# Where the attention scores of ten heads stand in TensorE's order: in front of the previous head's value products

## The chip, the core and the metric

The kernel runs on one core of a Trainium2 chip. A core has five engines, each with an instruction stream of its own that it works through in order: TensorE (PE in the profile, with its weight loads shown apart as PEld), VectorE (DVE), ScalarE (ACT), GpSimd (POOL) and SyncE (SP). TensorE multiplies, VectorE and ScalarE do the elementwise work, and in this kernel SyncE issues the loads of the weights while GpSimd issues the small transfers that turn data around. Engines wait for each other by semaphores. The metric is the device time of one execution in microseconds, lower is better.

## The reference

The kernel computes one decoder layer on a sequence of 256 tokens and 2048 channels, in float32. Cut to what matters here:

```python
h = rmsnorm(x)                                     # 256 x 2048
q_a, c_kv, k_rope, z_mla, c_in, b_gate, c_gate, z_conv, g_mla, g_conv = split(h @ w_in)
q = rmsnorm(q_a) @ w_q_b                           # 16 heads x (128 + 64 rotary)
kv = rmsnorm(c_kv) @ w_kv_b                        # 16 heads x (128 key + 128 value)
sc = (q_nope @ k_nope.T + q_rope @ k_rope.T) / sqrt(192)
attn = softmax(causal(sc)) @ v                     # per head, 256 x 128
attn = attn * silu(z_mla)
conv = short_conv(c_gate * c_in, 3 taps)
y_conv = (b_gate * conv * silu(z_conv)) @ w_o_conv
merged = sigmoid(g_mla) * (attn @ w_o_mla) + sigmoid(g_conv) * y_conv
out = x + rmsnorm(merged @ w_out)
```

## The kernel before

Every product is made of three passes: each float32 operand is split into a high part (`hi`) and the rest (`lo`), and `hi*hi`, `hi*lo` and `lo*hi` are added in PSUM. So every weight that arrives (tile `raw`) is first split: ScalarE copies it into `whi` (line 243), and VectorE subtracts to get `wlo` (line 244). Both steps are `split_act`, and the same function splits the queries, keys, values and probabilities.

The weights come as units of 128 x 2048 elements, in one list in the order in which they are used. `take(i)` hands unit i to the matmuls and has unit i+1 split. The halves of the split units live in five rotating buffers for `whi` and five for `wlo`, so the split of a half waits until TensorE has read the half five places before.

The middle of the program is a loop over the 16 heads h. `at = h % 4` is the place of a head among four and `v = h // 4` counts those fours. What TensorE does in one head, in order:

- if `at` is 0: four units of the gate `z` for these four heads (`gates`). From the second four on, the probabilities of the head before are brought in and split during the second of these units (`turn`), and during the third come that head's value products (`values(h - 1, pt)`) and the values of the next four heads (`make("v", v)`);
- the scores of head h, `score(h)` (line 812; for head 0 after the first `channels` unit, for the last head within the head before, line 824);
- `channels(h, 0)` and `channels(h, 1)`: two of the four units of a 512-column block of the convolution branch, which has nothing to do with the attention. They accumulate in two PSUM banks with the tag `cv`;
- `turn(h - 1)` (split of the previous head's probabilities, no matmul), `channels(h, 2)`, and `values(h - 1, pt)`;
- `make(...)`: in an even head the rotary queries of the next two heads (`group_r`), in an odd head their queries and keys (`group_a`, tiles `qn` and `kn`; one buffer each, for two heads);
- `channels(h, 3)`, after which `channels_done` empties the two `cv` banks. In heads with `at` 1 this is a VectorE instruction for each bank (line 716), in heads with `at` 0 and 2 one of ScalarE (lines 714 and 718).

A score is eight short matmuls (lines 607 to 613). The first of them multiplies the query by the keys' high and low parts together:

```python
mm(o, qn[0][:, j, t0], kn[:, :, j, :P], start=True, stop=False)
```

After the scores comes the softmax of that head: ScalarE copies half of the scores out of PSUM (line 618), VectorE adds the halves and the mask and finds the maxima (lines 619 to 627), ScalarE takes exponentials (line 630), VectorE divides and transposes blocks of 32 x 32 (lines 634 to 637, and 318 in `turned`). Then four transfers of GpSimd's queue write the tile to memory in turned order (`go`, line 326), and one brings it back (`come`, line 330). `come` isn't issued at once but put on the list `coming`; `arrive()` takes the oldest entry from the list and issues it. GpSimd issues its transfers in program order, so one that waits holds up those behind it.

`group_a` ends in this, for the keys: TensorE's result goes through `whole` (ScalarE line 393, VectorE line 394) to the tile `f`, and `split_act` makes `kn` from it (ScalarE line 243 for the high part, VectorE line 244 for the low part).

All matmuls stay in the order in which the program gives them (the wrapper `matmul`), and so does whatever stands in `tc.keep_in_program_order`. All other instructions, among them most of VectorE's and ScalarE's, are put in order by a scheduler at build time, which goes by its own estimate of when each would be ready. So a change in the program's order can move instructions on engines that the change doesn't name.

ScalarE holds the table of one set of functions at a time. The exponential of the softmax and the sigmoid of the gates need different ones, and where one follows the other the build puts a table load in between.

Of the kernel before, what the change touches and what calls it, by code (L numbers as in the profile page):

```python
# [23 lines left out]
H = 16  # L24
# [58 lines left out]
def tile_layer(ctx: ExitStack, tc: tile.TileContext, xw, w0, xb, x, pos, pvec, post_g, wc, wz, wcv, wkr, wqk, wqr, wv, cwr, wsq, out):  # L83
# [129 lines left out]
    def take(i):  # L213
        ahead(i)
        parts = splits.pop(i)

        def piece(j, n):
            o = j * n
            h, o = o // HALF, o % HALF
            return parts[h][0][:, o : o + n], parts[h][1][:, o : o + n]  # L220

        return piece

    def bank(name, tag="mm", bufs=4):
        return psum.tile([P, 512], F32, name=name, tag=tag, bufs=bufs)
# [80 lines left out]
    def temp(name, shape=(P, S), dt=F32, bufs=2, tag=None):  # L306

        tag, n = tag or name.rstrip("0123456789_"), shape[-1]
        if n % LINE == 0:
            return bp.tile(list(shape), dt, name=name, tag=tag, bufs=bufs)  # L310
        return bp.tile([P, -(-n // LINE) * LINE], dt, name=name, tag=tag, bufs=bufs)[:, :n]
# [78 lines left out]
    def whole(dst, ps):  # L390

        t = temp("half")
        nc.scalar.activation(t[:, :], ps[:, S:], AF.Copy)
        nc.vector.tensor_tensor(dst, ps[:, :S], t[:, :], op=ALU.add)
# [98 lines left out]
    def latent_split(name, both, g):  # L493

        f = lat_f[name].rearrange("p t (i k x) -> p k t i x", i=4, k=KR)
        for k in range(KR):
            hi, lo = (both[:, k, o : o + S].rearrange("p (t i x) -> p t i x", t=NT, i=4) for o in (0, S))
            tc.keep_in_program_order(nc.scalar.activation(hi, f[:, k], AF.Copy, scale=col(g, k)))
            tc.keep_in_program_order(
                nc.vector.scalar_tensor_tensor(lo, f[:, k], col(g, k), hi.bitcast(F32), op0=ALU.mult, op1=ALU.subtract)  # L500
            )
# [33 lines left out]
    def key_rope():  # L535
        rows(kr_f)
        rope(kr_f, kr_f, True)
        split_act(kr[:, 0, :], kr[:, 1, :], kr_f)
# [57 lines left out]
    def make(i, j):  # L596
        {"a": group_a, "r": group_r, "v": group_v}[i](j)
# [44 lines left out]
    def turn(p):  # L642

        pt = temp("pt", (P, 2, 3 * P), F32R, 1)
        hi, lo = (pt[:, j : j + 1, :].rearrange("p o (k q) -> p (o k) q", k=3) for j in range(2))
        split_act(quarters(hi), quarters(lo), by_rows(p[:, :], 3), True)
        return pt

    def values(h, pt):
        vv = groups["v", h // HV]  # L650
        j = h % HV
        o = bank(f"o{h}", tag="o", bufs=1)
        vs = slice(j * DV, (j + 1) * DV)
        both = o[:, :].rearrange("p (i q) -> p i q", i=2)
        mm = matmul
        mm(both, vv[0][:, 0, vs], pt[:, :, :S], start=True, stop=False)
        mm(o[:, :S], vv[1][:, 0, vs], pt[:, 0, :S], start=False, stop=False)
        mm(o[:, P:S], vv[1][:, 1, vs], pt[:, 0, S:], start=False, stop=False)
        mm(both[:, :, P:], vv[0][:, 1, vs], pt[:, :, S:], start=False, stop=True)

        at = at_t[:, h // HV, :, :].rearrange("p t (i k x) -> p t i k x", i=4, k=HV)[:, :, :, j, :]
        f = temp("f")
        whole(f[:, :], o)
        nc.vector.tensor_tensor(at, f[:, :].rearrange("p (t i x) -> p t i x", t=NT, i=4), at, op=ALU.mult)
# [5 lines left out]
    def quarter(pss, w, i):  # L670

        for t in range(NT):
            for k4 in range(4):
                k = 4 * i + k4
                a = [x_both[:, k, o + t * P : o + (t + 1) * P] for o in (0, S)]
                product(pss[t][:, :], a, w(k4, 512), k == 0, k == KD - 1)

    def gates(v, i):
        if i == 0:
            z_ps["now"] = [bank(f"z{v}_{t}") for t in range(NT)]  # L680
        quarter(z_ps["now"], take(u_gate[v][i]), i)

    def gates_done(v):
        for t in range(NT):
            ps, g, r = z_ps["now"][t], at_t[:, v, t, :], r_col[:, t : t + 1]
            nc.scalar.activation(g, ps[:, :], AF.Sigmoid, scale=r)
            now = nc.vector.scalar_tensor_tensor(g, ps[:, :], r, g, op0=ALU.mult, op1=ALU.mult)
            if v == 0:
                tc.keep_in_program_order(now)

    def gates_turn(v, t):
        g = at_t[:, v, t, :]
        go, come = turned(g, temp("cw", (P, 512), bufs=2), 4)
        go()
        return lambda: come(g)
# [5 lines left out]
    def channels(h, i):  # L701

        if i == 0:
            cv_ps["now"] = [bank(f"cv{h}_{t}", tag="cv", bufs=2) for t in range(NT)]
        quarter(cv_ps["now"], take(u_head[h][i]), i)
        if i == 3:
            channels_done(*divmod(h, 4))

    def channels_done(j, n):
        for t in range(NT):  # L710
            ps, r = cv_ps["now"][t], r_col[:, t : t + 1]
            w, u = cv_w[:, t, :], cv_t[:, j, t, :]
            if n == 0:
                nc.scalar.activation(u, ps[:, :], AF.Copy, scale=r)
            elif n == 1:
                nc.vector.scalar_tensor_tensor(u, ps[:, :], r, u, op0=ALU.mult, op1=ALU.mult)
            elif n == 2:
                nc.scalar.activation(w, ps[:, :], AF.Copy, scale=r)
            else:
                g = temp("cg", (P, 512), bufs=1)  # L720
                nc.scalar.activation(g[:, :], ps[:, :], AF.Sigmoid, scale=r)
                nc.vector.scalar_tensor_tensor(g[:, :], ps[:, :], r, g[:, :], op0=ALU.mult, op1=ALU.mult)
                nc.vector.tensor_tensor(w, w, g[:, :], op=ALU.mult)
# [48 lines left out]
    def arrive():  # L772
        coming.pop(0)()

    def score(h):
        ps_by_head[h], come = scores(h)
        coming.append(come)

    for h in range(H):
        v, at = divmod(h, HV)  # L780

        if at == 0:
            for i in range(4):
                gates(v, i)
                if v == 0 and i == 0:
                    ckv_come()
                elif v == 0 and i == 1:
                    next(table_parts)
                    key_rope()
                elif v == 0 and i == 2:  # L790
                    latent_split("qa", qa, "q_g")
                elif v and i == 0:
                    arrive()
                elif v and i == 1:
                    pt = turn(ps_by_head.pop(h - 1))
                    next(tap)
                elif v and i == 2:
                    values(h - 1, pt)
                    make("v", v)
            if v:  # L800
                next(tap)
            else:
                latent_split("ckv", ckv, "kv_g")
            gates_done(v)
        if h == 0:

            ahead(u_grp["r", 0])
            for i in first:
                make(*i)
            channels(h, 0)  # L810
        if h < H - 1:
            score(h)
        if h:
            channels(h, 0)
        if at == 0:
            coming.append(gates_turn(v, 0))
        channels(h, 1)
        if at == 0:
            arrive()
            coming.append(gates_turn(v, 1))  # L820
        else:
            pt = turn(ps_by_head.pop(h - 1))
        if h == H - 2:
            score(h + 1)

        if at == 2 or h == H - 1:
            next(tap)
        if at and h < H - 1:
            arrive()
        channels(h, 2)  # L830
        if at:
            values(h - 1, pt)
        else:
            arrive()
            if v:
                coming.append(channels_join(v - 1, 0))
        for i in made[h]:
            make(*i)
        if h == H - 1:
            pt = turn(ps_by_head.pop(h))  # L840
        channels(h, 3)
        if at == 2 or h == H - 1:
            next(tap)
        while coming and h < H - 1:
            arrive()
        if h == H - 1:
            values(h, pt)
        if at == 3:
            coming.append(channels_join(v, 1))
        if at == 1:  # L850
            tap = taps(v, 1)
            next(tap)
        elif at == 3 and h + 1 < H or h == H - 2:
            tap = taps(v, 0)
            next(tap)
# [280 lines left out]
```

## Time and profile before

| | |
|---|---|
| median of three runs | 1035.66 us (1035.56 to 1035.92) |
| the profiled execution's own time | 1034.93 us |
| span of the profile (first to last instruction) | 1033.2 us |
| TensorE busy | 1026.7 us (99%), 4680 matmuls |
| VectorE busy | 682.9 us (66%) |
| ScalarE busy | 526.7 us (51%) |
| GpSimd busy | 179.8 us (17%) |
| granted TensorE clock, mean | 0.999 of full speed |

In the profile's lines, `L244` is line 244 of the kernel before; `wlo<-raw,whi` means that the instruction writes the tile `wlo` from `raw` and `whi`, with buffer numbers left out. In a timeline each row has the start, the duration (both in us), the engine, the line and operation, the tiles and shapes, and how many instructions are merged into it; in brackets stands how long the engine had been idle before and what ended that. All matmuls have line 88, the wrapper, and are told apart by their tiles: `cv` is `channels`, `sc` the scores, `o` the value products, `qn` and `kn` queries and keys, `z` the gates. Matmuls overlap, so what a matmul costs TensorE is the distance to the start of the next.

### The profile page before, as it was taken

The page shows a single profiled execution, that of the slowest core. Times are in us where ns is not written, and L with a number is a line of the kernel's source. Part 1 is how long each engine was busy: PE and PEld are TensorE (multiplying, and loading weights), DVE is VectorE, ACT ScalarE, POOL GpSimd, SP SyncE. Part 2 cuts the span into 40 slices and gives each one's busy share as a digit, 9 for nine tenths or more (in the row PEclk, how much of TensorE's full clock was granted, in tenths as well). Part 3 has the DMA queues.
Part 4 walks back from the last instruction along what each step waited for, and adds up shares of the span by engine and source line. Part 5 has one row for each costly group of instructions (what it writes and reads, how often), then busy time and mean ns, then how long its engine had stood idle before and what let it go on. Part 6 is the DMA issues. An engine that isn't in the chain of part 4 may idle for free.

```text
span 1033.2 us, 12728 instructions
## 1 busy us (share of the span) xinstructions
PE 1026.7 (99%) x4680; PEld 855.0 (83%) x4680; DVE 682.9 (66%) x957; ACT 526.7 (51%) x734; POOL 179.8 (17%) x344
## 2 busy tenths in 40 slices
PE   9999999999999999999999999999999999999997
PEld 7888888888888888888888888888888888888886
DVE  7588777777787777767767785564455455455562
ACT  7766545555455454564555565344434444443551
POOL 4640421104201142112413120020010001002000
PEclk9999999999999999999999999999999999999999
DMA  9775766568565775856766765565565556558642
GB/s 359 281 252 215 267 236 215 204 220 284 194 254 186 232 283 187 278 179 244 264 236 225 258 222 201 204 223 190 199 217 208 189 202 242 180 189 336 230 167 81
DMA packets 44670, 233.25 MB, mean 226 GB/s; under 512 B 7968, under 2 KB 10656, under 8 KB 21696
## 3 DMA queue, kind: packets, MB, share of 16 engines
q1 hardware_dynamic: 32544, 199.67, 54.2%
q0 software_dynamic: 11632, 29.48, 8.8%
q10 hardware_dynamic: 432, 3.29, 0.8%
q8 instruction: 36, 0.59, 0.2%
q14 instruction: 26, 0.21, 0.1%
HBM read 215.66 MB, written 12.58 MB: 221 GB/s over the span
## 4 chain that ended last, share of the span: by engine, by line
PE 99%; DVE 0%; ACT 0%; issue 0%
PE cv L88 34%; PE sq L88 34%; PE out L88 8%; PE z L88 8%; PE qa L88 2%; PE qn L88 2%; PE kn L88 2%; PE vv L88 2%; PE ckv L88 2%; PE sc L88 1%; PE qr L88 1%; PE o L88 1%; PE idle L88 0%; PE kr L88 0%; DVE og L989 0%; ACT junk L970 0%
## 5 line engine op out<-in xcount | busy, mean ns | idle before, releaser
L244 DVE TENSOR_TENSOR wlo<-raw,whi 128x1024 fp32r<-128x1024 f32 (+1 forms) x370 | 440.4, 1197 | 284.2 <-ACT whi L243 273.5
L243 ACT ACTIVATE whi<-raw 128x1024 fp32r<-128x1024 f32 (+1 forms) x372 | 382.5, 1035 | 402.5 <-PE sq L88 180.5
L88 PE MATMUL cv<-whi,x_both 128*128 128x512 f32 x1024 | 321.1, 389 | 0.0
L88 PEld LDWEIGHTS cv<-whi,x_both 128*128 128x128 f32 x1024 | 192.3, 188 | 39.2
L88 PE MATMUL cv<-wlo,x_both 128*128 128x512 f32 x512 | 199.5, 390 | 0.0
L88 PE MATMUL sq<-whi,x_both 128*128 128x512 f32 x512 | 158.2, 389 | 0.0
L88 PEld LDWEIGHTS sq<-whi,x_both 128*128 128x128 f32 x512 | 96.1, 188 | 19.9
L88 PEld LDWEIGHTS cv<-wlo,x_both 128*128 128x128 f32 x512 | 96.2, 188 | 19.0
L88 PE MATMUL sq<-wlo,x_both 128*128 128x512 f32 x256 | 99.6, 389 | 0.0
L88 PE MATMUL z<-whi,x_both 128*128 128x512 f32 x256 | 80.0, 389 | 0.0
L88 PE MATMUL sq<-whi,at_both 128*128 128x512 f32 x256 | 79.4, 389 | 0.0
L88 PE MATMUL sq<-whi,cv_both 128*128 128x512 f32 x256 | 79.4, 389 | 0.0
L88 PE MATMUL out<-whi,m_both 128*128 128x512 f32 x256 | 79.0, 389 | 0.0
L326 POOL DMA_DIRECT2D far<-sg x32 | 17.5, 552 | 311.7 <-DVE sg L318 238.3
L326 POOL DMA_DIRECT2D far<-via x64 | 35.2, 557 | 183.8 <-DVE via L318 183.8
L88 PEld LDWEIGHTS out<-whi,m_both 128*128 128x128 f32 x256 | 48.0, 188 | 10.0
L88 PEld LDWEIGHTS sq<-wlo,x_both 128*128 128x128 f32 x256 | 48.0, 188 | 10.0
L88 PEld LDWEIGHTS z<-whi,x_both 128*128 128x128 f32 x256 | 48.0, 188 | 10.0
L88 PEld LDWEIGHTS sq<-whi,cv_both 128*128 128x128 f32 x256 | 48.0, 188 | 9.9
L88 PEld LDWEIGHTS sq<-whi,at_both 128*128 128x128 f32 x256 | 48.0, 188 | 9.9
L88 PE MATMUL z<-wlo,x_both 128*128 128x512 f32 x128 | 49.8, 389 | 0.0
L88 PE MATMUL sq<-wlo,at_both 128*128 128x512 f32 x128 | 49.8, 389 | 0.0
(216 smaller groups left out, 1126.2 us busy)
## 6 DMA issues: line engine op xcount, KB each, us to landing
raw<-wsq_dram SPq DMA_DIRECT2D x80, 1024.0 KB, 4.8
raw<-wcv_dram SPq DMA_DIRECT2D x64, 1024.0 KB, 5.6
raw<-wz_dram SPq DMA_DIRECT2D x16, 1024.0 KB, 4.9
raw<-wqk_dram SPq DMA_DIRECT2D x8, 1024.0 KB, 5.7
cw<-cwr_dram POOLq DMA_DIRECT2D x24, 256.0 KB, 5.8
raw<-wc_dram SPq DMA_DIRECT2D x4, 1024.0 KB, 9.9
raw<-wv_dram SPq DMA_DIRECT2D x4, 1024.0 KB, 5.4
far<-via POOLq DMA_DIRECT2D x64, 48.0 KB, 3.5
```

Source lines behind the costliest of these rows:

```text
L88: return tc.keep_in_program_order(nc.tensor.matmul(*a, **kw))
L243: a = nc.scalar.activation(hi, src, AF.Copy)
L244: b = nc.vector.tensor_tensor(lo, src, hi.bitcast(F32), op=ALU.subtract)
L326: tc.keep_in_program_order(queue.dma_start(out=f[i], in_=m))
```

## The change

Scores that stood ahead of a head's first `channels` unit now stand, for ten heads, directly ahead of `values` of the head in front:

- heads 1, 3, 5, 7, 9, 11 and 13 (`at` 1 and 3): behind `channels(h, 2)`, so three units later than before;
- heads 4, 8 and 12 (`at` 0): within the gates, ahead of `values(h - 1, pt)`, so before the values of the four heads and the last unit of the gates are made;
- heads 0, 2, 6, 10, 14 and 15 keep their place.

The return transfers (`arrive()`) follow: for `at` 0 one is issued after `gates_done`, and the one behind `channels(h, 1)` is left for `at` 2 alone, so that those of `at` 1 and 3 are issued at the end of the head.

```diff
@@ gates of a new four, third unit
                 elif v and i == 2:
+                    score(h)
                     values(h - 1, pt)
                     make("v", v)
@@ after the gates
             gates_done(v)
+            if v:
+                arrive()
         if h == 0:
             ahead(u_grp["r", 0])
             for i in first:
                 make(*i)
-            channels(h, 0)
-        if h < H - 1:
+        if at == 2:
+
             score(h)
-        if h:
-            channels(h, 0)
+        channels(h, 0)
+        if h == 0:
+            score(h)
         if at == 0:
             coming.append(gates_turn(v, 0))
         channels(h, 1)
@@ third and fourth unit
-        if at and h < H - 1:
+        if at == 2:
             arrive()
         channels(h, 2)
+
+        if at in (1, 3) and h < H - 1:
+            score(h)
         if at:
             values(h - 1, pt)
```

## The prediction

> **What bounds the kernel now.** I read the page's sums first, then the chain of waits, then one table of busy times over the stretch that the change touches (heads 1 to 15).
>
> ```profile
> span 1033.2 us, 12728 instructions
> ...
> PE 1026.7 (99%) x4680; PEld 855.0 (83%) x4680; DVE 682.9 (66%) x957; ACT 526.7 (51%) x734; POOL 179.8 (17%) x344
> ...
> PE 99%; DVE 0%; ACT 0%; issue 0%
> ```
>
> ```profile
> 107.00:589.00 482.00, 482.00 (x2266) 404.06 (x2265) 360.70 (x577) 257.81 (x395) 110.41 (x203) 1.00 0.68 236
> ```
>
> TensorE is busy in all of these 482 us, at full clock (the 1.00), and its 99% are also the chain that ended last. So there is next to nothing to win by taking waits away here, and any wait that the change puts in front of a matmul is added to the time in full. Two questions are left: does the new order make the same matmuls cheaper, and does some operand now come after TensorE wants it?
>
> **The matmuls themselves.** None is added or removed; ten groups of eight short ones change place. Here is TensorE around the scores of head 6 (a row with x2 holds two matmuls):
>
> ```profile
> 271.57 0.62 PE L88 MATMUL cv<-whi,x_both 128*128 128x512 f32 x2
> ...
> 273.38 0.39 PE L88 MATMUL cv<-wlo,x_both 128*128 128x512 f32 x1
> 273.61 0.39 PE L88 MATMUL cv<-whi,x_both 128*128 128x512 f32 x1
> 273.83 0.28 PE L88 MATMUL sc<-kn,qn_hi 128*128 128x256 f32 x1
> ...
> 274.77 0.39 PE L88 MATMUL cv<-whi,x_both 128*128 128x512 f32 x1
> ...
> 276.62 0.62 PE L88 MATMUL cv<-whi,x_both 128*128 128x512 f32 x2
> ```
>
> The eight take 274.77 - 273.83 = 0.94 us. From 271.57 to 273.38, ahead of them, lie eight distances of `cv` matmuls in 1.81 us; from 274.77 to 276.62, behind them, eight in 1.85. So leaving short matmuls for long ones costs some 0.04 us. Values leave for long ones too; with both side by side ten such borders go, at most 10 x 0.04 = 0.4 us. A part stays, since the value products now start in that slower rhythm: I take half, -0.2 us.
>
> **Keys for heads 2, 6, 10 and 14.** These scores keep their place, but they have the least room of all. Their keys are made one `channels` unit earlier, in the odd head. VectorE, ScalarE around head 6 before:
>
> ```profile
> 262.20 2.53 DVE L244 TENSOR_TENSOR wlo<-raw,whi 128x1024 fp32r<-128x1024 f32 x2 [2.86 <-ACT whi L243]
> ...
> 269.85 0.76 DVE L244 TENSOR_TENSOR qn_lo<-f,qn_hi 128x256 fp32r<-128x256 f32 x2
> 270.52 0.96 DVE L394 TENSOR_TENSOR f<-kn,half 128x256 f32<-128x256 f32 x2
> 271.40 0.74 DVE L716 SCALAR_TENSOR_TENSOR cv_f<-cv,r_both,cv_f 128x512 f32<-128x512 f32 x1
> 272.06 0.75 DVE L244 TENSOR_TENSOR kn<-f,kn 128x256 fp32r<-128x256 f32 x2
> 273.77 1.23 DVE L244 TENSOR_TENSOR wlo<-raw,whi 128x1024 fp32r<-128x1024 f32 x1 [0.96 <-ACT whi L243]
> 274.91 0.74 DVE L716 SCALAR_TENSOR_TENSOR cv_f<-cv,r_both,cv_f 128x512 f32<-128x512 f32 x1
> 275.57 1.22 DVE L244 TENSOR_TENSOR wlo<-raw,whi 128x1024 fp32r<-128x1024 f32 x1
> ```
>
> ```profile
> 265.80 0.64 ACT L393 ACTIVATE half<-qn 128x256 f32<-128x256 f32 x2
> ...
> 270.97 0.96 ACT L243 ACTIVATE kn<-f 128x256 fp32r<-128x256 f32 x2 [1.14 <-DVE f L394]
> 272.68 1.06 ACT L243 ACTIVATE whi<-raw 128x1024 fp32r<-128x1024 f32 x1 [0.74 <-PE cv L88]
> ```
>
> The second `kn` is done at 272.81, the score starts at 273.83: 1.0 us of room. Now the softmax of heads 1, 5, 9 and 13 falls into just this stretch, and the scheduler has answered by reordering. This is VectorE's built order up to the scores of head 6, before and after (operation, tiles; the tail only):
>
> ```
> before                                after
> f<-kn (2x)                            cv_f<-cv5_0       (line 716, bank 0)
> cv_f<-cv5_0   (line 716, bank 0)      f<-kn (2x)
> kn<-f,kn (2x)                         wlo<-raw,whi      (unit 56, second half)
> wlo<-raw,whi  (unit 56, second half)  cv_f<-cv5_1       (line 716, bank 1)
> cv_f<-cv5_1   (line 716, bank 1)      kn<-f,kn (2x)
> wlo<-raw,whi  (unit 57, first half)   wlo<-raw,whi      (unit 57, first half)
> ```
>
> ScalarE's order changes alike: `whi` of unit 56's second half now stands ahead of the two `kn<-f`. The first score matmul waits for the first `kn<-f,kn`. Both things now ahead of it wait for TensorE: this `whi` for a buffer that `channels(5, 3)` reads until shortly before its end (released at 272.68), and line 716 for the last matmul of `channels(5, 3)`, which is the one directly ahead of the score. So TensorE must stop, however early the rest is:
>
> - `whi` from 272.68, `wlo` from 273.77, line 716 from 274.91, as before; all three hang on TensorE;
> - the first `kn` subtraction takes the place of the last `wlo` row, from 275.57, and lasts about 0.42 (two in 0.75 with overlap): 275.99;
> - TensorE was ready at 273.83: 2.16 us, about 2.2 with the signal.
>
> Heads 2 and 14, the first and last of the four, have the same distances, and the built order is the same in all four:
>
> ```profile
> 141.07 1.22 DVE L244 TENSOR_TENSOR wlo<-raw,whi 128x1024 fp32r<-128x1024 f32 x1
> ```
>
> ```profile
> 139.34 0.28 PE L88 MATMUL sc<-kn,qn_hi 128*128 128x256 f32 x1
> ```
>
> ```profile
> 544.57 1.22 DVE L244 TENSOR_TENSOR wlo<-raw,whi 128x1024 fp32r<-128x1024 f32 x1
> ```
>
> ```profile
> 542.83 0.28 PE L88 MATMUL sc<-kn,qn_hi 128*128 128x256 f32 x1
> ```
>
> 141.07 + 0.42 - 139.34 = 2.15; 544.57 + 0.42 - 542.83 = 2.16. Four stalls of 2.2 us: **+8.8 us**. The lower bound is a `wlo` that got out of the way: last `cv` matmul 273.61 + 0.39, line 716 0.74, `kn` 0.42 make 275.16, a stall of 1.33, in all 5.3. The upper bound needs the next step.
>
> **Does VectorE get there in time?** Six table loads are added in ScalarE's order: the exponentials of heads 4, 8, 12 now come before the gates' sigmoid, so the table is switched before them, back after them, and again for the exponentials of heads 5, 9 and 13, which is in the tight stretch.
>
> ```profile
> L630 ACT ACT_TABLE_LOAD x4 | 5.1, 1283 | 0.1
> ```
>
> ```profile
> 278.28 0.40 ACT L630 ACTIVATE p<-p,nb 128x128 f32<-128x128 f32 x1 [3.02 <-DVE nb L627]
> ...
> 279.08 0.18 ACT L630 ACTIVATION_READ_ACCUMULATOR p<-p,nb 128x1 f32 x1
> ...
> 280.12 0.50 ACT L243 ACTIVATE pt<-p 128x384 fp32r<-128x384 f32 x1
> ```
>
> ```profile
> 230.36 0.17 DVE L634 RECIPROCAL rs<-sm 128x2 f32<-128x2 f32 x1 [1.33 <-ACT p L630]
> ...
> 231.15 0.58 DVE L318 STREAM_TRANSPOSE via<-p 128x384 f32<-128x384 f32 x1
> ```
>
> On TensorE's times of head 6 before, in the new order: ScalarE's two copies of `qn` end at 266.44; load 1.28, 267.72; the exponentials 0.98 (278.28 to the end of the last read, 279.26), 268.70; VectorE's reciprocal to transpose 1.37 (230.36 to 231.73), 270.1; a `wlo` 1.14 from start to start, 271.2; two `qn_lo` 0.67, 271.9; line 716 0.66, 272.5; two `f` 0.88, 273.4. That is 0.4 us ahead of the `wlo` at 273.77. So the loads cost nothing by themselves, covered by that 0.4; each us more in this chain would be a us more of stall, in the three heads with a load.
>
> [...]
>
> **What is moved at no cost, and its cover.** Scores of heads 4, 8, 12: their keys lie ready long before.
>
> ```profile
> 193.23 0.41 DVE L244 TENSOR_TENSOR kn<-f,kn 128x256 fp32r<-128x256 f32 x1
> ```
>
> ```profile
> 222.52 0.27 ACT L618 ACTIVATE sc_half<-sc 128x128 f32<-128x128 f32 x1
> ```
>
> The keys are done at 193.64, head 4's scores end near 222; some two units (11 us) earlier they are still ready. The softmax (some 3 us of VectorE, 1.4 us of it in the rows from 230.36 to 231.73) and the loads make the `wlo` halves around it later. Their cover: unit 56's second half is made at 275.0 and belongs to `channels(6, 1)`, which begins 24 matmuls behind 274.77, at 280.2, and reads that half six matmuls later, at 281.6, so 6.6 us ahead; VectorE idles for buffers too (2.86 us ahead of 262.20). If that cover went, the next late thing would be a `wlo`.
>
> The probabilities of an odd head start on their way three units later but are wanted at the same place.
>
> ```profile
> far<-via POOLq DMA_DIRECT2D x64, 48.0 KB, 3.5
> ...
> p<-far POOLq DMA_DIRECT2D x16, 192.0 KB, 4.2
> ```
>
> Head 5: transposed 270.1; four issues on GpSimd of 0.56 each, landed by 270.1 + 0.3 + 2.2 + 3.5 = 276.1; return 4.2, 280.3. ScalarE wants them at 280.12 (the `pt` row), plus the stall 282.3; the value products stand a further `channels` unit behind. Behind the return in GpSimd's queue stand the transfers for the convolution's taps, which VectorE also uses only after that `pt`. Cost zero.
>
> Without a score in between, the next `channels` follows directly on line 714 or 718 emptying the banks. Tightest is head 1's second bank:
>
> ```profile
> 112.07 0.69 ACT L714 ACTIVATE cv_f<-cv,r_both 128x512 f32<-128x512 f32 x1
> ```
>
> ```profile
> 113.88 0.61 PE L88 MATMUL cv<-whi,x_both 128*128 128x512 f32 x2
> ```
>
> Empty at 112.76, written from 114.11 (the second of the two); 0.94 earlier leaves 0.4 us. Cost zero.
>
> **Sum**, on the profiled execution: 1034.93 + 8.8 - 0.2 = 1043.5. The median is 0.73 above it: **1044.3 us**.
>
> **Rivals.**
>
> VectorE comes late to the tight stretch (the 0.4 us is a sum of nine terms). Late by 1.4 us in four heads, so 1.0 beyond the 0.4, 4.0 more: 1048.3. For it: ScalarE's and VectorE's waits for each other there are many; against: the chain above is bounded by rows.
>
> Not slower: the built order doesn't stop TensorE, because the score's wait ends early. It would need the subtraction for `kn` ahead of line 716 of bank 1. Then only the border is left, 1035.66 - 0.2 to -0.4: 1035.4. It decides from 1.0 us of room upwards; against it stands the order above. A gain above 0.2% has no term at all.
>
> The wait is as forecast but `wlo` isn't in front: 4 x 1.33, 1040.8.
>
> Probabilities late: should the return take its longest and hold ScalarE for 2 us, `whi` halves are late by as much; buffers ahead cover it, so 1044.3 still, or 1 to 3 us more.
>
> **How the numbers follow.** 0.2% of this time is 2.1 us, about what a measurement can tell from no change. Forecast 0.81; late VectorE or probabilities 0.10; shorter wait 0.04; not slower 0.05 (within 0.2%, or below by an unseen effect 0.01). The range goes from the shorter wait, 1040.8, to the late VectorE's 1048.3. So faster 0.01, same 0.04, slower 0.95.
>
> **What would show it.** In the profile after: TensorE idle ahead of `sc<-kn,qn_hi`, four times, ended by VectorE's `kn`, each about 2.2 us and 8.8 together; 18 table loads in place of 12 at 1.28 us; no idle time ahead of `o`, `cv` or `z`. Wrong if there are stalls ahead of other tiles, or if those ahead of `sc` differ in heads 2 (no load) and 6 (load).

## The result, and the profile after

The changed kernel takes 1046.40 us (median of five runs, 1045.96 to 1046.52), the kernel before 1035.66 (five runs on the same chip, 1035.17 to 1035.92): a ratio of 1.0103, 95% interval 1.0088 to 1.0118. So it is slower, by 10.7 us. The profiled execution took 1046.45. First the page, its sums and its chain:

```profile
span 1044.7 us, 12732 instructions
...
PE 1029.7 (99%) x4680; PEld 857.1 (82%) x4680; DVE 680.4 (65%) x957; ACT 535.2 (51%) x740; POOL 179.5 (17%) x344
...
PE 98%; DVE 1%; ACT 1%; issue 0%
```

TensorE's 4680 matmuls are the same ones, but its busy time has grown by 3.0 us, and the chain that ended last now has a per cent each of VectorE and ScalarE in it. TensorE's waits say where (waited for, total us, times, longest):

```profile
PE sc L88 <- DVE kn L244: 8.6, 4, 2.1
```

Before the change this line is not there. Everything TensorE now waits for within the heads is VectorE's `kn`, four times, ahead of a score. The stretch of the heads (length, then busy time of TensorE, its loads, VectorE, ScalarE, GpSimd, then the clock) shows it as time missing from the first figure; before, it was busy all through:

```profile
107.00:600.50 493.50, 484.95 (x2270) 405.75 (x2269) 358.84 (x577) 266.29 (x401) 110.94 (x204) 1.00 0.67 231
```

The timeline round head 6, TensorE, then VectorE, then ScalarE:

```profile
278.04 0.39 PE L88 MATMUL cv<-wlo,x_both 128*128 128x512 f32 x1
278.26 0.39 PE L88 MATMUL cv<-whi,x_both 128*128 128x512 f32 x1
280.79 0.35 PE L88 MATMUL sc<-kn,qn_hi 128*128 128x256 f32 x1 [2.14 <-DVE kn L244]
280.99 0.22 PE L88 MATMUL sc<-kn,qn_lo 128*128 128x128 f32 x1
```

```profile
277.14 0.74 DVE L394 TENSOR_TENSOR f<-kn,half 128x256 f32<-128x256 f32 x2
278.43 1.23 DVE L244 TENSOR_TENSOR wlo<-raw,whi 128x1024 fp32r<-128x1024 f32 x1 [0.55 <-ACT whi L243]
279.57 0.75 DVE L716 SCALAR_TENSOR_TENSOR cv_f<-cv,r_both,cv_f 128x512 f32<-128x512 f32 x1
280.23 0.75 DVE L244 TENSOR_TENSOR kn<-f,kn 128x256 fp32r<-128x256 f32 x2
```

```profile
271.10 1.28 ACT L630 ACT_TABLE_LOAD   x1
272.40 0.40 ACT L630 ACTIVATE p<-p,nb 128x128 f32<-128x128 f32 x1
...
277.33 1.06 ACT L243 ACTIVATE whi<-raw 128x1024 fp32r<-128x1024 f32 x1 [1.85 <-PE cv L88]
278.30 0.71 ACT L243 ACTIVATE kn<-f 128x256 fp32r<-128x256 f32 x2
```

Read it from ScalarE upwards: `whi` waits 1.85 us for TensorE's `cv` matmuls to give its buffer back; VectorE's `wlo` waits 0.55 for `whi`; line 716 comes directly behind `wlo`, and the two `kn` behind line 716. The tiles `f` that the keys are made from were complete at 277.88, and ScalarE had their high parts by 279.01 (line 243, which comes behind `whi` itself), but the subtraction begins at 280.23. From 278.26 the last `cv` matmul takes 0.227 us of TensorE (the usual distance between these), so the score could have begun at 278.49 and began at 280.79, 2.30 later. The bracket's 2.14 is less because it counts from the matmul's modelled end (278.26 + 0.39).

One more thing stands in TensorE's timeline, behind the first of the four stops:

```profile
142.44 0.36 PE L88 MATMUL sc<-kn,qn_hi 128*128 128x256 f32 x1 [2.14 <-DVE kn L244]
...
143.48 0.63 PE L88 MATMUL cv<-whi,x_both 128*128 128x512 f32 x1
143.91 0.63 PE L88 MATMUL cv<-wlo,x_both 128*128 128x512 f32 x1
144.34 1.05 PE L88 MATMUL cv<-whi,x_both 128*128 128x512 f32 x2
...
146.88 0.62 PE L88 MATMUL cv<-whi,x_both 128*128 128x512 f32 x2
```

From 143.48 to 144.34 lie two `cv` matmuls, 0.43 us each where 0.227 is usual. The table by stretches (the clock is the figure behind the five engines) says why, and shows the second stop beside it:

```profile
140.01:143.42 3.41, 1.27 (x10) 1.01 (x9) 3.34 (x5) 1.59 (x4) 2.23 (x5) 1.00 0.49 116
143.42:146.84 3.42, 3.42 (x10) 2.72 (x9) 2.04 (x9) 1.26 (x5) 1.57 (x3) 0.50 0.97 317
146.84:150.25 3.41, 3.41 (x16) 2.80 (x15) 1.12 (x3) 0.88 (x1) 1.67 (x3) 1.00 0.95 238
276.55:279.96 3.41, 2.10 (x10) 1.41 (x8) 2.86 (x6) 2.62 (x4) 0.83 (x3) 1.00 0.19 46
279.96:283.38 3.42, 2.59 (x15) 2.36 (x16) 3.21 (x8) 0.28 (x1) 3.42 (x7) 1.00 0.81 268
```

For 3.42 us TensorE got half its clock. Eight `cv` matmuls went in that time (143.48 to 146.88, 3.40 us); at 0.227 they take 1.82. So the first stop cost 1.6 us more than its idle time. Behind the other three stops the clock stayed at 1.00.

The sum of the difference: four stops of 2.30 make 9.2; the first score matmul behind each takes 0.20 to the next (280.79 to 280.99) where an unstopped one takes 0.12 (an example stands with the first experiment), 0.3 in all; the halved clock 1.6. That is 11.1 against the 10.7 between the medians; what is left over, -0.4, lies within what the border between short and long matmuls was forecast to give back, but isn't shown to be that. Only one of the five runs was traced. That the others hold a halving too is suggested by their mean granted clock: it is 0.997 in all five, and 0.998 to 1.000 in the runs of the kernel before beside the experiments; half of 3.42 us is 0.0016 of the time.

### The profile page after: what moved, and what is told of

Same layout as the page of the kernel before. It is cut to its first block, busy times and chain, and to the rows that moved or that the text cites. A ratio compares the mean times of both kernels' runs of the same rounds, so it can differ in the third digit from the quotient of the medians.

```text
span 1044.7 us, 12732 instructions
## 1 busy us (share of the span) xinstructions
PE 1029.7 (99%) x4680; PEld 857.1 (82%) x4680; DVE 680.4 (65%) x957; ACT 535.2 (51%) x740; POOL 179.5 (17%) x344
## 4 chain that ended last, share of the span: by engine, by line
PE 98%; DVE 1%; ACT 1%; issue 0%
PE sq L88 33%; PE cv L88 33%; PE out L88 8%; PE z L88 8%; PE qa L88 2%; PE kn L88 2%; PE qn L88 2%; PE vv L88 2%; PE ckv L88 2%; PE sc L88 2%; PE qr L88 1%; PE o L88 1%; ACT whi L243 0%; PE idle L88 0%; PE kr L88 0%; DVE cv_f L716 0%
```

## Experiments

Before the first four ran, three explanations stood beside each other: the built order alone (A, that of the prediction), lateness by the softmax and the table loads in the tight stretch (B), and an effect of the chip's state at the start or of the clock by itself (C).

**All ten scores moved, the keys bound ahead.** The keys are put ahead on VectorE and ScalarE, and nothing else is changed: both instructions of line 716 and the second half of the unit that is split there may issue only behind the keys (`split_act` now returns its two instructions).

```diff
+    keys, tight = [], [u_head[h][1] for h in (2, 6, 10, 14)]
+    def behind_keys():
+        st = ExitStack()
+        for ins in keys:
+            st.enter_context(tc.issue_after(ins.ins))
+        return st
...
-            split_act(hi[:, :n], lo[:, :n], t[:, h : h + n], ...)
+            with behind_keys() if h and i in tight else ExitStack():
+                split_act(hi[:, :n], lo[:, :n], t[:, h : h + n], ...)
...
-                split_act(hi[:, j, :], lo[:, j, :], f[:, :])
+                keys[:] = split_act(hi[:, j, :], lo[:, j, :], f[:, :])
...
-                nc.vector.scalar_tensor_tensor(u, ps[:, :], r, u, op0=ALU.mult, op1=ALU.mult)
+                with behind_keys():
+                    nc.vector.scalar_tensor_tensor(u, ps[:, :], r, u, op0=ALU.mult, op1=ALU.mult)
```

> All ten scores stay moved and the six extra table loads stay; only the built order is bound: the split of the keys for heads 2, 6, 10 and 14 goes ahead of line 716 and of the following weight half, on VectorE and ScalarE. Theory A (TensorE stops because the keys stand behind two steps that themselves wait for TensorE): the keys are done some 0.5 us before TensorE wants them, no stall, 1035.66 - 0.3 = about 1035.3 us, granted clock 0.998 to 0.999. Rival B (the softmax and the table loads in that stretch make ScalarE and VectorE late): they are all still there, so the four stalls stay at 1.5 us or more each, 1041 us or more.

Measured: 1035.08 us (1034.22 to 1035.80) beside 1035.78 for the kernel before on the same chip, ratio 0.9992 [0.9984, 1.0001]. All 10.7 us are gone. TensorE's longest waits, then its timeline and VectorE's round head 6 (line numbers are eight to ten higher in this kernel: 252 is the subtraction, 726 is line 716):

```profile
PE fin L88 <- ACT dg L1028: 0.9, 1, 0.9
PE idle L88 <- PEq L1141: 0.8, 1, 0.8
```

```profile
274.96 0.28 PE L88 MATMUL sc<-kn,qn_hi 128*128 128x256 f32 x1
275.08 0.22 PE L88 MATMUL sc<-kn,qn_lo 128*128 128x128 f32 x1
```

```profile
273.85 0.76 DVE L252 TENSOR_TENSOR kn<-f,kn 128x256 fp32r<-128x256 f32 x2 [0.15 <-ACT kn L251]
274.53 1.40 DVE L726 SCALAR_TENSOR_TENSOR cv_f<-cv,r_both,cv_f 128x512 f32<-128x512 f32 x2
275.85 2.35 DVE L252 TENSOR_TENSOR wlo<-raw,whi 128x1024 fp32r<-128x1024 f32 x2
```

No wait ahead of `sc` is left. The softmax of head 5 and the table load are in front of these keys as in the changed kernel, and the first key is done at about 274.27 (273.85 and 0.42), 0.7 us ahead of the score. So B falls: the moved work fits, and only the order made it late.

**Only heads 1, 5, 9 and 13 moved.**

```diff
+MOVED = (1, 5, 9, 13)
...
-        if at in (1, 3) and h < H - 1:
+        if at in (1, 3) and h in MOVED:
             score(h)
...
-        if at == 2:
+        if 0 < h < H - 1 and h not in MOVED:
             score(h)
```

(and in the same way for the gates and for `arrive`)

> Only the scores of heads 1, 5, 9 and 13 move; 12 table loads as in the kernel before. Theory A: all four stalls are there, 2.30 us each plus some 0.08 for the first matmul behind: 1035.66 + 9.5 = 1045.2 us; where one of them halves TensorE's clock for 3.4 us as the first did in the changed kernel, 1.6 more each, so 1045 to 1047. Rival B with the loads as cause: without loads below 1040 us.

Measured: 1046.53 us (1045.92 to 1048.22), ratio 1.0105 [1.0091, 1.0119]. In this and the next two kernels lines are numbered one higher. Its wait and its table loads at the exponential:

```profile
PE sc L89 <- DVE kn L245: 8.6, 4, 2.1
```

```profile
L631 ACT ACT_TABLE_LOAD x4 | 5.1, 1283 | 0.1
```

The same four stops of the same size, with no table load added (four at this line, as before; the changed kernel has seven). So the loads neither make the stops nor lengthen them. They are not free on VectorE, though. Without a load it stands idle for 1.02 us ahead of the `wlo` in question, where 0.55 is left in the changed kernel:

```profile
276.59 1.22 DVE L245 TENSOR_TENSOR wlo<-raw,whi 128x1024 fp32r<-128x1024 f32 x1 [1.02 <-ACT whi L244]
```

So a load takes about 0.5 us of this idle time, and the stop doesn't feel it as long as some is left.

**Only the other six moved** (`MOVED = (3, 4, 7, 8, 11, 12)` in the same edit).

> The other six scores move (heads 3, 7, 11 and 4, 8, 12); 18 table loads. Theory A: no stall, 1035.66 less a little for six borders of short matmuls, 1035.4 us. Rival B with the loads as cause: 1037 us or more.

Measured: 1035.35 us (1034.49 to 1035.89), ratio 0.9996 [0.9987, 1.0005]. The first line of its waits is no longer a score:

```profile
PE qa L89 <- ACT whi L244: 1.0, 2, 0.6
```

These six moves, with all six added table loads, cost nothing that can be measured. The wait named is at the start of the program, before the heads.

**Only head 5 moved** (`MOVED = (5,)`): a single stop.

> Only the score of head 5 moves: one stall, ahead of the score of head 6. Theory A: 2.30 + 0.08, 1038.0 us if the clock stays, 1039.6 us if this stall halves it for 3.4 us. Rival C (what was lost beyond the four stalls is a slower start of the execution, 0.8 us in the changed kernel's profile, and has nothing to do with the stalls): 1038.0 us and full clock behind the stall in every run. Rival B: under 1037 us.

Measured: 1038.85 us, ratio 1.0028 [1.0016, 1.0039]. An effect that came with the start alone could not be cut to a quarter by moving one head, so C as the whole cause falls. But a stop of 2.4 is not 3.1, and the six runs lie in two groups of three: 1037.37, 1037.84, 1038.28, and 1039.42, 1040.10, 1040.11. The profiled one is of the upper group:

```profile
273.91:277.32 3.41, 1.37 (x7) 0.79 (x5) 2.38 (x5) 2.62 (x4) 1.16 (x3) 1.00 0.13 28
277.32:280.74 3.42, 3.32 (x12) 3.06 (x13) 2.35 (x6) 0.28 (x1) 2.62 (x5) 0.50 0.93 298
```

Its clock was halved behind the stop, again for 3.42 us. With 1.6 us for that the upper group stands where it should: 1035.78 + 2.3 + 0.1 + 1.6 = 1039.8. That the lower group is without a halving fits its 1038.2. None of its runs was traced, but the mean granted clock of each run agrees: 0.997 in the three upper ones, 0.999, 0.998 and 0.999 in the lower.

**When is the clock halved?** From the moment at which a trace first shows the full clock to a halving lies a whole number of equal steps: from 6.89 to 143.42 in the changed kernel 40 of 3.413 us; with heads 1, 5, 9, 13 moved 121 (4.31 to 417.32); with head 5 alone 80 (4.26 to 277.32). So the stretches shown above, which are cut at these steps, are those by which the clock seems to be granted. With heads 1, 5, 9 and 13 moved, the third and fourth stop:

```profile
413.90:417.32 3.42, 1.53 (x11) 1.47 (x12) 3.22 (x6) 1.33 (x3) 2.61 (x6) 1.00 0.62 178
417.32:420.73 3.41, 3.41 (x10) 2.65 (x9) 2.25 (x10) 0.99 (x4) 1.00 (x2) 0.50 1.00 312
550.44:553.85 3.41, 1.65 (x8) 1.03 (x6) 2.39 (x5) 2.62 (x4) 1.08 (x2) 1.00 0.18 41
553.85:557.27 3.42, 3.04 (x17) 2.74 (x18) 3.19 (x9) 0.28 (x1) 2.72 (x5) 1.00 0.93 294
```

Two stops of the same length: one leaves TensorE 1.53 us of work in its window and halves the next; the other leaves 1.65 and does not. To test this I held TensorE for other lengths, from the kernel without stops: the keys bound ahead, and the first key's subtraction done n times more, with the same result, in the four tight places.

```diff
                 keys[:] = split_act(hi[:, j, :], lo[:, j, :], f[:, :])
+            for _ in range(N if n == "kn" and g in (1, 3, 5, 7) else 0):   # N = 4, 8, 14
+                keys.append(nc.vector.tensor_tensor(lo[:, 0, :], fs0[:, :], hi[:, 0, :].bitcast(F32), op=ALU.subtract))
```

(`fs0` is the first key's `f`.)

> All ten scores moved and the keys bound ahead, as in the kernel that binds them; the subtraction for the first key tile is done four times over in heads 2, 6, 10 and 14 (0.34 us each, the result the same). The last then ends 274.61 + 4 x 0.34 + 0.07 = 276.04 on that kernel's times against a score ready at 274.96: four stops of 1.1 us, and 0.15 each for the bank emptied later. Theory W (the clock is judged in windows of 3.41 us that run freely from the moment it first reached full speed, and is halved for the next window when TensorE stood for about 1.9 us or more of one): 1.1 us never suffices, the clock stays 0.999, time 1035.1 + 4 x 1.25 = 1040.1. Rival R (any stop can cost the clock, by chance): halvings also here, each about 1.7 us more, runs spread by 1.7 or more.

> The same with eight repeats: stops of 2.4 us, a little more than in the changed kernel, made by another instruction. Without the clock 1035.1 + 4 x 2.55 = 1045.3. Theory W: a stop of 2.4 us puts 1.9 us into one window for some phases and not for others, so some runs halve the clock once or twice, each time for 3.41 us, which costs about 1.7: 1045 to 1050, runs some 1.7 apart, and in the trace a halving is there exactly where one window holds 1.9 us or more of the stop. Rival R: halvings bear no relation to these windows.

> The same with fourteen repeats: stops of 4.5 us. However the windows lie, one of them holds at least half of it, 2.2 us. Theory W: every stop halves the clock in every run, four times about 1.9 us on top of 4 x 4.65: 1035.1 + 18.6 + 7.6 = 1061.3, runs close together. Without a clock effect 1053.7; rival R: between the two, runs spread.

> The kernel with the ten scores moved and the keys bound ahead once more, for a narrower interval. If the border gain of 0.2 to 0.4 us is all that the move itself is worth: 1035.2 to 1035.5 beside 1035.7 before, no more than 0.04% apart. If the move is worth something beyond that (the first measurement gave a ratio of 0.9992), below 1035.0 again.

Measured, beside 1035.39 for the kernel before and 1035.16 for the kernel without stops (ratio 0.9998 [0.9990, 1.0007]):

| repeats | time, us | ratio | stops in the trace, us | halvings |
|---|---|---|---|---|
| 4 | 1040.73 (1040.57 to 1042.55) | 1.0054 [1.0040, 1.0067] | 1.02, 1.51, 1.50, 1.50 | none |
| 8 | 1052.98 (1051.32 to 1053.62) | 1.0167 [1.0153, 1.0181] | 2.86, 3.34, 3.34, 3.34 | three, of one window |
| 14 | 1069.31 (1068.04 to 1070.48) | 1.0327 [1.0313, 1.0341] | 5.62, 6.11, 6.10, 6.10 | four, of two windows |

The stops (start to start, less 0.227 for the `cv` matmul, as above) came out longer than planned, since a repeat takes 0.45 us and not 0.34; this is VectorE with eight repeats (line 580 is the repeat):

```profile
278.25 3.63 DVE L580 TENSOR_TENSOR kn<-f,kn 128x256 fp32r<-128x256 f32 x8
```

So the times forecast for these three were too low. The first stop is about 0.5 us shorter in each because its keys come earlier: in the first experiment's kernel their subtraction starts 1.60 us ahead of head 2's score (no table load) and 1.11 ahead of head 6's (a load). What the three tell apart is in the windows. With four repeats the emptiest window of the four stops:

```profile
412.12:415.53 3.41, 2.07 (x14) 1.60 (x13) 3.31 (x8) 2.01 (x3) 0.57 (x1) 1.00 0.23 59
```

With eight, the third and fourth stop:

```profile
419.14:422.55 3.41, 1.16 (x9) 1.19 (x10) 3.27 (x8) 0.16 (x1) 0.17 (x2) 1.00 0.20 58
422.55:425.96 3.41, 3.41 (x10) 2.62 (x9) 3.41 (x8) 0.28 (x1) 3.16 (x6) 0.50 0.65 135
555.67:559.09 3.42, 1.92 (x9) 1.26 (x7) 3.13 (x9) 2.76 (x4) 1.09 (x2) 1.00 0.18 43
559.09:562.50 3.41, 1.73 (x12) 1.63 (x13) 3.31 (x7) 0.28 (x1) 0.62 (x2) 1.00 0.20 58
562.50:565.90 3.40, 3.40 (x17) 2.81 (x15) 3.14 (x8) 0.19 (x1) 2.60 (x5) 1.00 0.73 195
```

The fourth is 3.34 us long, as the third is, but falls across a boundary, leaves 1.92 and 1.73 us of work in its two windows, and the clock stays. So the length of a stop doesn't decide by itself, and the halvings are not without relation to the windows (rival R): they follow what is left in one window. R had also named a spread of 1.7 us or more as its sign, and with four repeats the runs do spread by 2.0. But the slowest, 1042.55, is the traced one, without a halving (its excess lies at the start, last section), and the next, 1041.96, has a mean clock of 1.000, which leaves no room for one. With fourteen repeats every stop halves the clock, as theory W had forecast, but for two windows where W had one; the fourth, with the first halved windows of the other three:

```profile
142.83:146.24 3.41, 0.73 (x3) 0.77 (x4) 3.24 (x8) 0.00 (x0) 0.00 (x0) 0.50 0.00 0
286.19:289.60 3.41, 1.61 (x7) 1.64 (x8) 3.31 (x7) 0.00 (x0) 0.51 (x1) 0.50 0.00 0
429.55:432.96 3.41, 2.08 (x9) 2.11 (x10) 3.34 (x6) 0.00 (x0) 0.97 (x2) 0.50 0.01 2
572.91:576.32 3.41, 2.34 (x10) 2.28 (x11) 3.34 (x6) 0.26 (x1) 1.23 (x3) 0.50 0.01 1
576.32:579.74 3.42, 3.42 (x10) 2.65 (x9) 2.52 (x7) 0.84 (x5) 1.99 (x4) 0.50 0.89 234
```

The times agree with what is lost in this way. Eight repeats: waits of 12.2 us by the profile and 0.16 more for each by starts, 12.8; 0.3 for the four first score matmuls; three halvings of 1.6; together 17.9, measured 1052.98 - 1035.16 = 17.8. Fourteen: waits of 23.3 and 0.6, again 0.3; half of the 6.8 us in the four partly filled windows is 3.4, and half of four full ones 6.8; together 34.4, measured 34.2.

## Why the prediction was right

**The bound.** Right: TensorE is never idle in the stretch before, so each wait put ahead of a matmul shows in the time. Binding the keys ahead takes all of it away.

**Four stops ahead of the scores of heads 2, 6, 10 and 14.** Right in place, number and cause: VectorE's `kn` ends them, `whi`, `wlo` and line 716 stand ahead, and `whi` waits for TensorE. Line 716 hangs on TensorE too, as the prediction says, but doesn't wait for it in the trace: its matmul ends at 278.65, and it starts at 279.57, when `wlo` lets it. So the length of the stop comes from the wait of `whi` and the work behind it. Sized 2.2 each, measured 2.30. The missing 0.1 lies between the end of the first subtraction and the start of the score. The prediction's "signal", some 0.04 in its 2.2, was an estimate; measured it is 280.79 - (280.23 + 0.42) = 0.14 (the `kn` subtractions take 0.42 each, 416 ns in the median of the sixteen). Moreover the first score matmul behind a stop takes 0.08 longer, a term that wasn't in the sum. Together 0.7 us over the four.

**Table loads at no cost.** Right for the time. ScalarE has 18 where it had 12, seven instead of four at the exponential and four instead of one at line 686:

```profile
L630 ACT ACT_TABLE_LOAD x7 | 9.0, 1283 | 0.1
L686 ACT ACT_TABLE_LOAD x4 | 5.1, 1283 | 0.1
```

The load at 271.10 is 1.28 long, and VectorE still stood idle 0.55 us ahead of the `wlo` at 278.43 (forecast 0.4). Heads 2 (no load in the stretch) and 6 (a load) both show 2.14 in their brackets, as the forecast wanted. And with heads 1, 5, 9 and 13 alone there are four equal stops without an added load. In the changed kernel a load stands at 222.78 ahead of the exponentials of head 4, one at 225.08 ahead of the gates' sigmoid, and the one at 271.10 ahead of the exponentials of head 5. Each load lasts 1283 ns, and the exponential behind the one at 271.10 starts at 272.40, 0.02 us after its end. What a load does take is about 0.5 us of VectorE's idle time (the experiment with heads 1, 5, 9 and 13), and enough was left.

**What was moved at no cost.** Right: six heads by themselves change the time by a ratio of 0.9996 [0.9987, 1.0005].

**The border gain of 0.2 us.** Not to be told: with the keys bound ahead the two measurements give 0.9992 [0.9984, 1.0001] and 0.9998 [0.9990, 1.0007], gains of 0.7 and 0.2 us between the medians, and both intervals take in no gain at all.

**What the sum lacked.** The clock. The sum took every matmul to run at full speed behind a stop; one of the four stops in the traced run halved it for 3.42 us, which cost 1.6 us. The sum of 1044.3 with +0.1 on each stop, 0.3 for the first score matmuls and one halving is 1046.6, measured 1046.4. So the forecast came within its range because the terms it lacked are small, and the upper bound (a late VectorE, 1048.3) covered them by another mechanism, which did not occur. In this part it was luck.

**The rivals.** VectorE late: no, the 0.55 us of idle time. The shorter wait of 1.33: no, `wlo` stood ahead all four times. Not slower: this is what the first experiment made, by the very condition that the rival named (the subtraction ahead of line 716), and its 1035.4 was then measured as 1035.1 and 1035.2. Probabilities late: no, TensorE has no wait ahead of `o`.

## What to carry to other kernels

Where one engine is never idle, read the built order of the others behind a change, not only the lines that it edits: here ten moved groups cost nothing, and a reordering of a few instructions of VectorE and ScalarE, which the change doesn't name, cost all 10.7 us. Look above all for an operand whose producer has come to stand behind an instruction that waits for its own consumer; such a stop is as long as the chain from there (here 2.30 us), however early everything else is. And price a stop of TensorE like these with a possible stretch of halved clock behind it, here 1.6 us: behind stops of 2.3 us some had one, behind stops of 1.5 none. Lengths in between were not measured.

## What the runs showed of the hardware

**The clock can fall behind a stop of 2.3 us.** In these traces, a window of 3.41 us that still held 1.53 us of TensorE's work or less (1.53, 1.37, 1.27, 1.16, and less with the longer holds) was followed by one at half clock, and a window at full clock with 1.65 or more (1.65, 1.73, 1.92, 2.07, 2.10) was not. Whether 2.3 us of idle time fall into one window or across two depends on where the windows lie, which changes from run to run (the first full clock came at 4.26 us in one trace and at 9.33 in another); the two groups of runs with head 5 alone moved, 2 us apart, fit this. The length of a stop alone did not decide: 1.9 us of idle time in one window (heads 1, 5, 9 and 13 moved, the third stop) were enough, and 3.34 across two (eight repeats, the fourth) were not.

**Coming back.** At half clock a window with 3.32 us of matmuls (head 5 alone) or more brought the full clock back, one with 2.34 or less did not (fourteen repeats). Halved, those are 1.66 and 1.17 us of full-speed work, above the 1.65 and below the 1.53 that stand on either side at full clock; that one measure holds both ways would fit these few stops, but they do not settle it.

**The start varies.** The full clock began at 4.33 us in the profile before and at 6.89 in the one after. In the same stretch TensorE did eleven matmuls and seven, before, then after:

```profile
4.33:6.89 2.56, 2.56 (x11) 1.72 (x11) 2.44 (x5) 1.18 (x4) 0.00 (x0) 1.00 1.01 338
```

```profile
4.33:6.89 2.56, 2.55 (x7) 1.87 (x7) 2.47 (x6) 0.78 (x2) 0.00 (x0) 1.00 1.01 367
```

The 1.00 in the second of these is no reading: the trace has no record of the clock ahead of the first full one, and the table then shows 1.00. The pace tells it, since from 5.13 to 6.83 the matmuls after the change start 0.43 us apart, as in the halved window. Four matmuls of 0.227 are 0.9 us, and they are lost ahead of everything that the change touches; with four repeats, in the profiled run, the slowest of its five, the full clock came at 9.33. Comparing two spans by the microsecond needs this term taken out first: 1044.7 - 1033.2 is 11.5, of which 0.9 lie here.
